# A two-layer transformer kernel: gate weights loaded first, later loads moved back, gate-row and key products over 128 rows

## The chip, the cores and the metric

The kernel runs on one core of one Trainium2 chip. The metric is the device time of one execution in microseconds (us). Before the change the median of three runs is 2478.57 us (2474.83 to 2481.1).

TensorE (PE) multiplies, with its weight loads shown as PEld; VectorE (DVE), ScalarE (ACT) and GpSimd (POOL) do the elementwise work; SyncE (SP) issues nearly all transfers (DMAs). Each engine works through its instructions in order.

## The reference, cut to what matters

The model has an mLSTM layer, a retrieval feed-forward layer, an attention layer, a second retrieval layer and a last hybrid layer with a feed-forward part. The change lies in the first: a gated recurrence over 256 tokens with 8 heads, query and key of 64 and value of 128 numbers a head.

```python
proj = x @ w_in                    # q, k, v, gates, output gate
ig = gate_i + b_if[0]; lf = log_sigmoid(gate_f + b_if[1])
b = cumsum(lf)
log_w = where(causal, b[t] - b[s] + ig[s], -inf)
m_t = maximum(log_inter, max(log_w, -1))
w = exp(log_w - m_t)
qk = einsum('bhtd,bhsd->bhts', q, k) * w
num = qk @ v + ...;  den = sum(qk) + ...
h = num / maximum(abs(den), exp(-m_t))
hn = layer_norm_per_head(h) * hn_g
out = (sigmoid(og) * hn) @ w_out
```

The kernel does all 256 tokens of a head at once: with M the running maximum of ig - b, the weight of source s for target t is exp(ig[s] - b[s] - M[t]) below the diagonal.

## The kernel before

Matrices are multiplied nearly in fp32 by splitting each operand into a rounded half (type fp32r, `hi`, by an ACT copy) and the rest (`lo`, by a subtraction on DVE or, where a call asks for it, POOL). `mm3` (lines 157 to 161) then makes three products: hi x hi, hi x lo, lo x hi. A weight slab of 1 MB comes from memory into one of three `raw` buffers (`prep`, line 131), is split in two parts into pools of 8 `hi` and 7 `lo` buffers, and is used by `linT` (weights stationary, output transposed) or `linN` (x stationary). A scheduler orders each engine's instructions by what is ready and by program order; pools decide when a load may start.

The mLSTM stage, `mlstm` (line 414), runs so:
- `load_x` (line 405) loads the transposed x in four pieces of 256 KB, each split in two. `trig_tables` (line 804) follows: rotation angles, needed much later, with a load of the positions, eight DVE operations and a sine on ACT.
- The gate weights (one slab of 512 KB) and four query/key slabs of 1 MB each go through `linT` with 24 and 4 x 48 products of 256 columns. Between them the gate chain runs on ACT and DVE over 32 rows (lines 447 to 469): absolute value, exponential, logarithm, a running sum (`Bc`), a running maximum (`M`), and both gate rows into `ab2`.
- Two PE transposes (line 481) turn `ab2` into per-token columns `tok`. Then `linN` makes the value product of four slabs, with 96 products of 512 columns (line 485); its `lo` halves are made on POOL.
- For each head, `head_a` (line 493) makes the gate rows: a fp32 product of the selector `sel` (8 rows, -1 in row h) with `M`, plus the causal mask, and a fp32 product of 64-row key and query. `head_b` (line 506) multiplies by the values and normalises. Products of the output gate and, later, of the output weights stand between the heads. `norm_heads` (line 529) normalises four heads and transposes them.
- `post_norm` (line 239) adds the residual and normalises; at its end the gain and shift rows `gr` and `br` (lines 283, 284) are applied on DVE. The retrieval layer begins with the slabs of `peer_w_q`.

The pool `mlw` holds two buffers each of the heads' work tiles and stays open to the end of the stage.

Of the kernel before, what the change touches and what calls it, by code (L numbers as in the profile page):

```python
# [17 lines left out]
OP = mybir.AluOpType  # L18
# [33 lines left out]
class Builder:  # L52
# [43 lines left out]
    def setup(self):  # L96
# [4 lines left out]
        nc.sync.dma_start(self.vecs, self.A["vecs"])  # L101
# [29 lines left out]
    def prep(self, name, s, lo_engine=None):  # L131
# [6 lines left out]
        self.nc.sync.dma_start(raw, src)  # L138
# [266 lines left out]
def load_x(B):  # L405
    nc = B.nc
    B.x32 = B.t(B.state, [P, KD, S], F32, "x32")
    for k in range(0, KD, 2):
        nc.sync.dma_start(B.x32[:, k:k + 2, :], B.A["xT"][:, k:k + 2, :])
        for i in range(k, k + 2):  # L410
            B.split(B.x32[:, i, :], B.xT[0][:, i, :], B.xT[1][:, i, :])


def mlstm(B):
# [4 lines left out]
    with B.pool("ml") as p, B.pool("mlw", 2) as w:  # L419
        for n, i in (("a_w_gate", 0), ("a_w_qk", 0)):  # L420
            B.prep(n, i, nc.gpsimd if i else v)
        nc.sync.dma_start(B.X, A["x"])
        qT = B.t(p, [P, 4, S], F32, "qT")
        kT = B.t(p, [P, 4, S], F32, "kT")
# [3 lines left out]
        sel = B.t(p, [8, 8, P], F32, "sel")  # L428
        nc.gpsimd.memset(sel, 0.0)
        nc.gpsimd.affine_select(out=sel, in_=sel, pattern=[[1, 8], [0, P]], compare_op=OP.not_equal, fill=-1.0,  # L430
                                base=0, channel_multiplier=-1)
        v.memset(va[:, :, :, 128:129], 1.0)
        hn = B.t(p, [P, D], F32, "hn")
        nc.sync.dma_start(hn, A["hn_g"].to_broadcast([P, D]))
        nc.gpsimd.tensor_scalar(hn, hn, 0.5, None, op0=OP.mult)
# [12 lines left out]
        e = B.t(p, [32, S], F32, "e")  # L448
# [10 lines left out]
        zero = B.t(p, [32, S], F32, "zero")  # L459
        v.memset(zero, 0.0)  # L460
# [17 lines left out]
        tok = B.t(p, [P, 2, 64], F32, "tok")
# [6 lines left out]
        acc = B.linN(B.xT, "a_w_v", lo_engine=nc.gpsimd)  # L485
# [7 lines left out]
        def head_a(h):  # L493
            r0, c = 64 * (h % 2), h // 2
            qk, lw = B.psum(), B.psum()
            ex = B.t(w, [P, 3 * P], F32, "ex")
            for sb in range(2):
                o = slice(sb * S, sb * S + S - sb * P)
                mm(lw[:, o], sel[:, h, :], M[0:8, sb * P:], start=True, stop=False)
                mm(lw[:, sb * S:sb * S + P], B.ident_b, B.smask_b, start=False, stop=True)  # L500
                mm(qk[:, o], kT[r0:r0 + 64, c, sb * P:(sb + 1) * P], qT[r0:r0 + 64, c, sb * P:], start=True, stop=True)
                act(ex[:, o], lw[:, o], AF.Exp, bias=tok[:, sb, h:h + 1])
            v.tensor_tensor(ex, ex, qk[:, :3 * P], op=OP.mult)
            pt[h] = ex
# [66 lines left out]
        B.accN(acc, [(oT, B.slab("a_w_out", s), 2 * s, 2) for s in (2, 3)], False, True)  # L571
        with B.pool("rows") as rows:
# [231 lines left out]
def trig_tables(B):  # L804
# [3 lines left out]
    with B.pool("tr") as p:  # L808
# [711 lines left out]
def build(tc, A, out, stages=ALL):  # L1520
    with ExitStack() as ctx:
# [56 lines left out]
```

## Time and profile before

| | |
|---|---|
| median of 3 runs | 2478.57 us |
| profiled execution | 2474.93 us, span 2472.0 us |
| PE busy | 2373.6 us, 96% of the span |
| DVE, ACT, POOL busy | 1627.4, 1230.4, 346.4 us |
| read and written | 457.99 and 34.60 MB |

Busy time of PE counts pipelined products from their start to their modelled end, so the spacing of starts says more than the duration of one. The granted clock (PEclk) is a share of 2.4 GHz: 0.50 is 1.2 GHz. A row of a timeline gives start, duration, engine, line, operation and tiles (output <- inputs), and in brackets the idle time of that engine before it and what ended it.

### The profile page before, as it was taken

Reading aid. Unit: us, or ns where it says so; the run is one execution under the profiler, and the core shown is the slowest. Engines: PE = TensorE matmul, PEld = TensorE weight load, DVE = VectorE, ACT = ScalarE, POOL = GpSimd, SP = SyncE. Lnnn points to the kernel's source line nnn. Section 1 sums busy time; section 2 is a strip of 40 time slices with the busy share of each in tenths; the row PEclk is TensorE's granted clock in tenths of the full one; section 3 lists DMA queues with packets and bytes.
Section 4 is the critical chain, followed back from the end, with each engine's and each line's share of the span. In section 5 each row is a group of like instructions: output and inputs, shape, how many; then the busy total and the mean of one; then the engine's idle time right before and its main releaser. Section 6 shows DMA issues by size and latency. Waiting matters only on the chain. (4 is left out here: it accounts for less than half of the span.)

```text
span 2472.0 us, 40796 instructions
## 1 busy us (share of the span) xinstructions
PE 2373.6 (96%) x16430; PEld 2167.0 (88%) x16430; DVE 1627.4 (66%) x3069; ACT 1230.4 (50%) x1813; POOL 346.4 (14%) x212
## 2 busy tenths in 40 slices
PE   7989999999999999989989999999999989999998
PEld 6779898889999998978989888999999888789998
DVE  5469995786666665656999566555555573459554
ACT  5455555444444444645455444444444464455442
POOL 5345000000000001445300000000000131313000
PEclk9989999999999999999999999999999999999999
DMA  7334577887677664433367766656655344224543
GB/s 258 120 110 150 226 282 268 293 326 264 251 263 273 255 227 148 154 137 131 144 239 280 258 236 218 227 200 208 218 208 201 137 162 160 81 86 161 198 149 108
DMA packets 134204, 495.22 MB, mean 200 GB/s; under 512 B 8064, under 2 KB 76032, under 8 KB 80896
## 3 DMA queue, kind: packets, MB, share of 16 engines
q1 hardware_dynamic: 129120, 458.55, 51.8%
q10 hardware_dynamic: 4896, 34.08, 3.4%
q8 instruction: 128, 2.10, 0.3%
q14 instruction: 60, 0.49, 0.1%
HBM read 457.99 MB, written 34.60 MB: 199 GB/s over the span
## 5 line engine op out<-in xcount | busy, mean ns | idle before, releaser
L78 ACT ACTIVATE hi<-raw 128x1024 fp32r<-128x1024 f32 (+1 forms) x754 | 771.3, 1044 | 838.8 <-PE ps L160 336.8
L129 DVE TENSOR_TENSOR lo<-raw,hi 128x1024 fp32r<-128x1024 f32 (+1 forms) x634 | 778.0, 1234 | 420.6 <-PE ps L161 254.2
L159 PE MATMUL ps<-s,hi 128*128 128x256 f32 x3248 | 923.5, 285 | 16.3 <-ACT hi L78 13.8
L160 PE MATMUL ps<-s,hi 128*128 128x256 f32 x3248 | 924.2, 285 | 2.1 <-DVE s L276 1.5
L161 PE MATMUL ps<-s,lo 128*128 128x256 f32 x3248 | 921.0, 284 | 5.3 <-DVE lo L129 5.3
L159 PEld LDWEIGHTS ps<-s,hi 128*128 128x128 f32 x3248 | 617.4, 190 | 22.6 <-ACT hi L78 14.2
L160 PEld LDWEIGHTS ps<-s,hi 128*128 128x128 f32 x3248 | 618.3, 190 | 7.4 <-issue 2.2
L161 PEld LDWEIGHTS ps<-s,lo 128*128 128x128 f32 x3248 | 617.9, 190 | 7.3 <-DVE lo L129 7.3
L129 POOL TENSOR_TENSOR lo<-raw,hi 128x1024 fp32r<-128x1024 f32 (+1 forms) x120 | 292.4, 2455 | 1340.6 <-ACT hi L78 1148.9
L159 PE MATMUL acc<-hi,ah 128*128 128x512 f32 x1024 | 400.6, 391 | 9.6 <-ACT ah L78 9.5
L160 PE MATMUL acc<-lo,ah 128*128 128x512 f32 x1024 | 401.0, 392 | 0.0
L161 PE MATMUL acc<-hi,al 128*128 128x512 f32 x1024 | 400.1, 391 | 0.0
L159 PEld LDWEIGHTS acc<-hi,ah 128*128 128x128 f32 x1024 | 193.1, 189 | 49.1 <-ACT ah L78 10.8
L161 PEld LDWEIGHTS acc<-hi,al 128*128 128x128 f32 x1024 | 193.0, 189 | 41.2 <-DVE al L129 0.7
L160 PEld LDWEIGHTS acc<-lo,ah 128*128 128x128 f32 x1024 | 193.0, 188 | 37.9
L129 DVE TENSOR_TENSOR al<-aw,ah 128x512 fp32r<-128x512 f32 x128 | 88.2, 689 | 54.9 <-ACT ah L78 54.8
L78 ACT ACTIVATE ah<-aw 128x512 fp32r<-128x512 f32 x128 | 80.1, 626 | 71.3 <-DVE aw L789 62.5
L789 DVE TENSOR_TENSOR aw<-g,wt 128x256 f32<-128x256 f32 x156 | 59.3, 422 | 39.4 <-ACT g L78 39.4
L756 PE MATMUL ps<-oh,o 128*128 128x128 f16 x512 | 65.1, 219 | 11.5 <-DVE oh L750 5.0
L78 ACT ACTIVATE st<-ps 128x512 f32<-128x512 f32 x128 | 66.6, 604 | 1.6 <-ACT pre L78 1.6
L78 ACT ACTIVATE g<-ps 128x512 f32<-128x512 f32 (+1 forms) x82 | 46.5, 567 | 39.1 <-PE ps L161 39.1
L757 PE MATMUL ps<-ol,o 128*128 128x128 f16 x512 | 64.7, 218 | 0.0
(461 smaller groups left out, 2433.6 us busy)
## 6 DMA issues: line engine op xcount, KB each, us to landing
raw<-in_peer_u SPq DMA_DIRECT2D x128, 1024.0 KB, 4.9
raw<-in_peer_v SPq DMA_DIRECT2D x128, 1024.0 KB, 4.9
wd<-st ACTq DMA_DIRECT2D x32, 1024.0 KB, 4.5
wt<-wd SPq DMA_DIRECT2D x32, 1024.0 KB, 6.1
raw<-in_w_ada SPq DMA_DIRECT2D x24, 1024.0 KB, 5.3
raw<-in_peer_w_q SPq DMA_DIRECT2D x16, 1024.0 KB, 4.9
raw<-in_ffn_gate SPq DMA_DIRECT2D x11, 1024.0 KB, 4.8
raw<-in_ffn_up SPq DMA_DIRECT2D x11, 1024.0 KB, 4.8
```

The source lines that it names most:

```text
L78: i = self.nc.scalar.activation(out, in_, func, **kw)
L129: (lo_engine or self.nc.vector).tensor_tensor(lo, src, hi.bitcast(F32), op=OP.subtract)
L159: mm(out, lhsT[0], rhs[0], start=first, stop=False)
L160: mm(out, lhsT[0], rhs[1], start=False, stop=False)
L161: mm(out, lhsT[1], rhs[0], start=False, stop=last)
L756: mm(ps[:, i * P:(i + 1) * P], o2[:, t // 2, :, t % 2], oh1[:, t // 2, :, t % 2], start=True, stop=False)
L757: w_last = mm(ps[:, i * P:(i + 1) * P], o2[:, t // 2, :, t % 2], ol1[:, t // 2, :, t % 2], start=False, stop=True)
L789: v.tensor_tensor(aw[:, sl].rearrange("p (g t) -> p g t", t=16), g[:, sl].rearrange("p (g t) -> p g t", t=16), wt[:, :, (j % 4) * 2 + i, : ...
```

## The change

- The load of the gate weights is issued first, on ACT's queue (`nc.scalar`) instead of SP's, from within `load_x`. The small constants `vecs` are loaded between the second and the third piece of x.
- The loads of the residual x, of the head gain `hn` and of the positions, with the rotation tables, come after the value product in program order; the two transposes of `ab2` as well. `hn` is scaled on DVE instead of POOL, and the value slabs' `lo` halves are made on DVE.
- The selector has 128 rows and type fp32r; `M` is split into two fp32r halves `Mp`, in 128 rows of which 32 are filled and the others zero. So one fp32 product over 8 rows becomes two fp32r products over 128 rows.
- Each head has a key tile of its own of 128 rows, of which the 64 of the other head are zero; the product with `qT` runs over 128 rows, still in fp32.
- Some tiles share memory (`e` with `ab`, `M` with `u`, `n` with `pi`, a one-column `zero`), and `mlw` is closed before `post_norm`, whose rows take its space.

```diff
@@ setup
-        nc.sync.dma_start(self.vecs, self.A["vecs"])
@@ prep
-    def prep(self, name, s, lo_engine=None):
+    def prep(self, name, s, lo_engine=None, queue=None):
-        self.nc.sync.dma_start(raw, src)
+        (queue or self.nc.sync).dma_start(raw, src)
@@ load_x
+    B.prep("a_w_gate", 0, None, nc.scalar)
     for k in range(0, KD, 2):
         nc.sync.dma_start(B.x32[:, k:k + 2, :], B.A["xT"][:, k:k + 2, :])
+        if k == 2:
+            nc.sync.dma_start(B.vecs, B.A["vecs"])
@@ mlstm
-    with B.pool("ml") as p, B.pool("mlw", 2) as w:
-        for n, i in (("a_w_gate", 0), ("a_w_qk", 0)):
-            B.prep(n, i, nc.gpsimd if i else v)
-        nc.sync.dma_start(B.X, A["x"])
+    with B.pool("ml") as p, ExitStack() as es:
+        w = es.enter_context(B.pool("mlw", 2))
+        B.prep("a_w_qk", 0)
-        kT = B.t(p, [P, 4, S], F32, "kT")
+        kT = B.t(p, [P, 8, S], F32, "kT")
+        nc.gpsimd.memset(kT, 0.0)
-        sel = B.t(p, [8, 8, P], F32, "sel")
-        nc.gpsimd.memset(sel, 0.0)
-        nc.gpsimd.affine_select(out=sel, in_=sel, ...
+        sel = B.t(p, [P, 8, P], F32R, "sel")
+        Mp = B.t(p, [P, 2, S], F32R, "Mp")
+        s32 = B.t(B.hi_p, [P, 8, P], F32, "hi")
+        nc.gpsimd.memset(s32, 0.0)
+        v.memset(Mp.bitcast(F32), 0.0)
+        nc.gpsimd.affine_select(out=s32, in_=s32, ...
+        act(sel, s32, AF.Copy)
-        hn = B.t(p, [P, D], F32, "hn")
-        nc.sync.dma_start(hn, A["hn_g"].to_broadcast([P, D]))
-        nc.gpsimd.tensor_scalar(hn, hn, 0.5, None, op0=OP.mult)
...
-        M = B.t(p, [32, S], F32, "M")
+        M = u
         v.tensor_tensor_scan(M, ab2[0:32, :], zero, 0.0, op0=OP.max, op1=OP.max)
+        B.split(M, Mp[0:32, 0, :], Mp[0:32, 1, :])
...
-                act(kT[:, c - 4, :], ps, AF.Copy, scale=0.125)
+                for r0 in (0, 64):
+                    act(kT[r0:r0 + 64, 2 * (c - 4) + r0 // 64, :], ps[r0:r0 + 64, :], AF.Copy, scale=0.125)
         B.linT(B.xT, "a_w_qk", range(4), ev_qk)
+        acc = B.linN(B.xT, "a_w_v")
+        trig_tables(B)
+        nc.sync.dma_start(B.X, A["x"])
+        hn = B.t(p, [P, D], F32, "hn")
+        nc.sync.dma_start(hn, A["hn_g"].to_broadcast([P, D]))
+        v.tensor_scalar(hn, hn, 0.5, None, op0=OP.mult)
...
-        acc = B.linN(B.xT, "a_w_v", lo_engine=nc.gpsimd)
...
-                mm(lw[:, o], sel[:, h, :], M[0:8, sb * P:], start=True, stop=False)
+                for i in range(2):
+                    mm(lw[:, o], sel[:, h, :], Mp[:, i, sb * P:], start=i == 0, stop=False)
-                mm(qk[:, o], kT[r0:r0 + 64, c, sb * P:(sb + 1) * P], qT[r0:r0 + 64, c, sb * P:], ...
+                mm(qk[:, o], kT[:, h, sb * P:(sb + 1) * P], qT[:, c, sb * P:], ...
...
+        es.close()
         with B.pool("rows") as rows:
@@ build
-        trig_tables(B)
         if "a0" in stages:
             mlstm(B)
```

On SP, at the start of the program before (`raw` is a weight slab, `s` the residual x, `pi` the positions, `gr` a row of the norm):

```order
L101 DMA vecs_84<-in_vecs 128x185
L409 DMA x_17_117<-in_xT 128x512 x4
L138 DMA raw_164<-in_a_w_gate 128x1024
L138 DMA raw_170<-in_a_w_qk 128x2048
L810 DMA pi_142<-in_positions 128x256
L422 DMA s_15_115<-in_x 128x2048
L138 DMA raw_298<-in_a_w_qk 128x2048
L138 DMA raw_359<-in_a_w_qk 128x2048
L434 DMA hn_192<-in_hn_g 128x1024
L138 DMA raw_420<-in_a_w_qk 128x2048
L283 DMA gr_1336<-in_ln_g 128x1024
```

SP at the same place after the change:

```order
L409 DMA x_17_116<-in_xT 128x512 x2
L411 DMA vecs_84<-in_vecs 128x185
L409 DMA x_17_116<-in_xT 128x512 x2
L137 DMA raw_150<-in_a_w_qk 128x2048
L137 DMA raw_279<-in_a_w_qk 128x2048
L137 DMA raw_340<-in_a_w_qk 128x2048
L137 DMA raw_403<-in_a_w_qk 128x2048
L824 DMA pi_610<-in_positions 128x256
L487 DMA s_15_114<-in_x 128x2048
```

The positions and the residual x now stand behind all query/key slabs, and the gate weights have left this queue. The row loads `gr` and `br` stand further on:

```order
L137 DMA raw_1471<-in_peer_w_q 128x2048
L137 DMA raw_1563<-in_peer_w_q 128x2048
L282 DMA gr_1361<-in_ln_g 128x1024
L283 DMA br_1362<-in_ln_b 128x1024
L137 DMA raw_1655<-in_peer_w_q 128x2048
```

Before, `gr` was the eleventh load and `br` stood among the output-gate slabs.

ACT at its start after the change (`s` are the rounded x pieces, `raw_117` the gate slab, `ab` and `lf` belong to the gate chain):

```order
L137 DMA raw_117<-in_a_w_gate 128x1024
L78 ACT_TABLE_LOAD
L78 ACTIVATE s_13_112<-x_17_116 128x256
L78 ACTIVATE hi_119<-raw_117 128x1024
L78 ACTIVATE s_13_112<-x_17_116 128x256 x7
L78 ACTIVATE hi_152<-raw_150 128x1024
L78 ACTIVATE hi_156<-raw_150 128x1024
L78 ACTIVATE ig_176<-ps_178,vecs_84 32x256
L78 ACTIVATE z_177<-ps_178,vecs_84 32x256
L78 ACTIVATE ab_205<-z_177 32x256
L78 ACTIVATE ab_205<-ab_205 32x256
L78 ACTIVATE sel_166<-hi_168 128x1024
```

Next stand a table load, the logarithm `lf`, and only then the split of the second query/key slab. Before, the gate split stood behind all eight x pieces.

PE at the first two heads before (`acc` are output-gate products):

```order
L499 MATMUL ps_642<-M_243,sel_186 128x256
L500 LDWEIGHTS ident_b_88
L500 MATMUL ps_642<-smask_b_91,ident_b_88 128x128
L501 MATMUL ps_641<-qT_181,kT_182 128x256
L501 MATMUL ps_641<-qT_181,kT_182 128x128
L499 MATMUL ps_654<-M_243,sel_186 128x256
L499 MATMUL ps_642<-M_243,sel_186 128x128
```

and after:

```order
L494 MATMUL ps_633<-ident_79,ab_43_218 128x64
L512 MATMUL ps_650<-Mp_167,sel_166 128x256 x2
L513 LDWEIGHTS ident_b_87
L513 MATMUL ps_650<-smask_b_90,ident_b_87 128x128
L514 MATMUL ps_649<-qT_160,kT_161 128x256
L514 MATMUL ps_649<-qT_160,kT_161 128x128
L512 MATMUL ps_664<-Mp_167,sel_166 128x256 x2
```

The transposes of `ab2` now stand directly ahead of the heads, and each gate-row product is a pair.

## Rows read from the trace of the kernel before

**Rows 1.** The page, busy time of one engine: us, share, instructions.

```profile
PE 2373.6 (96%) x16430; PEld 2167.0 (88%) x16430; DVE 1627.4 (66%) x3069; ACT 1230.4 (50%) x1813; POOL 346.4 (14%) x212
```

**Rows 2.** Timeline of all engines, 0 to 12 us: start, us, engine, line, operation.

```profile
4.74 1.42 ACT L78 ACTIVATE s<-x 128x256 fp32r<-128x256 f32 x4 [2.66 <-DMA x<-in_xT]
5.19 1.46 DVE L129 TENSOR_TENSOR s<-x,s 128x256 fp32r<-128x256 f32 x4 [4.11 <-ACT s L78]
...
8.23 0.72 ACT L78 ACTIVATE s<-x 128x256 fp32r<-128x256 f32 x2 [0.50 <-DMA x<-in_xT]
...
9.51 1.06 ACT L78 ACTIVATE hi<-raw 128x1024 fp32r<-128x1024 f32 x1 [0.55 <-DMA raw<-in_a_w_gate]
...
10.60 1.23 DVE L129 TENSOR_TENSOR lo<-raw,hi 128x1024 fp32r<-128x1024 f32 x1 [0.74 <-ACT hi L78]
```

**Rows 3.** Timeline of PE, 10 to 26 us.

```profile
10.62 0.58 PE L159 MATMUL ps<-s,hi 128*128 128x256 f32 x1 [10.62 <-ACT hi L78]
...
16.73 0.39 PE L159 MATMUL ps<-s,hi 128*128 128x256 f32 x1
...
22.41 0.28 PE L161 MATMUL ps<-s,lo 128*128 128x256 f32 x1
24.56 0.38 PE L159 MATMUL ps<-s,hi 128*128 128x256 f32 x1 [1.87 <-ACT hi L78]
...
25.82 0.39 PE L161 MATMUL ps<-s,lo 128*128 128x256 f32 x1 [0.76 <-DVE lo L129]
```

**Rows 4.** Timeline of ACT, 22 to 29 us.

```profile
22.48 0.47 ACT L78 ACTIVATE ig<-ps,vecs 32x256 f32<-32x256 f32 x1
...
28.18 1.28 ACT L78 ACT_TABLE_LOAD   x1
```

**Rows 5.** Timeline of all engines, 35 to 50 us.

```profile
35.37 16.39 POOL L129 TENSOR_TENSOR lo<-raw,hi 128x1024 fp32r<-128x1024 f32 x6 [5.70 <-DVE lf L458]
...
37.14 2.44 DVE L465 TENSOR_TENSOR ab<-ig,Bc 32x256 f32<-32x256 f32 x1
```

**Rows 6.** Timeline of PE, 47 to 48 us.

```profile
47.29 0.31 PE L481 MATMUL ps<-ident,ab 64*128 64x64 f32 x2 [3.42 <-POOL lo L129]
47.53 0.68 PE L159 MATMUL acc<-hi,s 128*128 128x512 f32 x1
```

**Rows 7.** Stretches: length, PE, PEld, DVE, ACT, POOL, PEclk, DMA share, GB/s.

```profile
49.00:51.00 2.00, 2.00 (x7) 1.54 (x6) 0.00 (x0) 1.07 (x2) 2.00 (x2) 0.50 0.94 377
76.00:78.00 2.00, 2.00 (x7) 1.43 (x7) 0.39 (x1) 0.37 (x1) 0.00 (x0) 0.50 0.68 283
100.00:108.00 8.00, 8.00 (x40) 6.22 (x39) 7.74 (x25) 3.86 (x7) 2.55 (x1) 1.00 0.29 106
```

**Rows 8.** Timeline of PE, 71 to 83 us.

```profile
71.47 0.69 PE L499 MATMUL ps<-M,sel 8*128 8x256 f32 x2
...
75.01 0.80 PE L159 MATMUL acc<-hi,s 128*128 128x512 f32 x1
...
82.04 0.40 PE L161 MATMUL acc<-hi,s 128*128 128x512 f32 x1
...
82.96 0.61 PE L511 MATMUL ps<-va,ex 128*128 128x129 f32 x4
```

**Rows 9.** Timeline of PE, 83 to 86 us: one head.

```profile
83.72 0.69 PE L499 MATMUL ps<-M,sel 8*128 8x256 f32 x2
84.35 0.23 PE L500 MATMUL ps<-smask_b,ident_b 128*128 128x128 bf16 x1
...
85.36 0.48 PE L499 MATMUL ps<-M,sel 8*128 8x128 f32 x2
85.77 0.23 PE L500 MATMUL ps<-smask_b,ident_b 128*128 128x128 bf16 x1
```

**Rows 10.** Timeline of SP, 100 to 165 us.

```profile
104.38 30.92 SPq L138 DMA_DIRECT2D raw<-in_peer_w_q  x4
```

**Rows 11.** Timeline of DVE, 100 to 165 us.

```profile
160.75 2.61 DVE L286 TENSOR_TENSOR s<-s,gr 128x1024 f32<-128x1024 f32 x2
```

More of the change, by code (lines that the diff above doesn't have):

```diff
@@ L427, in mlstm @@
         H = B.t(p, [P, 2, 8, P], F32, "H")
-        sel = B.t(p, [8, 8, P], F32, "sel")
-        nc.gpsimd.memset(sel, 0.0)
-        nc.gpsimd.affine_select(out=sel, in_=sel, pattern=[[1, 8], [0, P]], compare_op=OP.not_equal, fill=-1.0,
+        sel = B.t(p, [P, 8, P], F32R, "sel")
[3 more added lines that the diff above has]
+        v.memset(Mp.bitcast(F32), 0.0)
+        nc.gpsimd.affine_select(out=s32, in_=s32, pattern=[[1, 8], [0, P]], compare_op=OP.not_equal, fill=-1.0,
                                 base=0, channel_multiplier=-1)
+        act(sel, s32, AF.Copy)
         v.memset(va[:, :, :, 128:129], 1.0)
-        hn = B.t(p, [P, D], F32, "hn")
-        nc.sync.dma_start(hn, A["hn_g"].to_broadcast([P, D]))
-        nc.gpsimd.tensor_scalar(hn, hn, 0.5, None, op0=OP.mult)
         bif = B.vec("b_if")
@@ L447, in mlstm @@
         ab = B.t(p, [32, S], F32, "ab")
-        e = B.t(p, [32, S], F32, "e")
+        e = ab
         u = B.t(p, [32, S], F32, "u")
@@ L458, in mlstm @@
         v.scalar_tensor_tensor(lf, z, 0.0, lf, op0=OP.min, op1=OP.subtract)
-        zero = B.t(p, [32, S], F32, "zero")
-        v.memset(zero, 0.0)
+        zero1 = B.t(p, [32, 1], F32, "zero")
+        v.memset(zero1, 0.0)
+        zero = zero1.to_broadcast([32, S])
         ab2 = B.t(p, [64, S], F32, "ab2")
@@ L493, in head_a @@
         def head_a(h):
-            r0, c = 64 * (h % 2), h // 2
+            c = h // 2
             qk, lw = B.psum(), B.psum()
@@ L498, in head_a @@
                 o = slice(sb * S, sb * S + S - sb * P)
-                mm(lw[:, o], sel[:, h, :], M[0:8, sb * P:], start=True, stop=False)
+                for i in range(2):
+                    mm(lw[:, o], sel[:, h, :], Mp[:, i, sb * P:], start=i == 0, stop=False)
                 mm(lw[:, sb * S:sb * S + P], B.ident_b, B.smask_b, start=False, stop=True)
-                mm(qk[:, o], kT[r0:r0 + 64, c, sb * P:(sb + 1) * P], qT[r0:r0 + 64, c, sb * P:], start=True, stop=True)
+                mm(qk[:, o], kT[:, h, sb * P:(sb + 1) * P], qT[:, c, sb * P:], start=True, stop=True)
                 act(ex[:, o], lw[:, o], AF.Exp, bias=tok[:, sb, h:h + 1])
@@ L811, in trig_tables @@
         ang = B.t(p, [P, S], F32, "ang")
-        n = B.t(p, [P, S], F32, "n")
         v.tensor_copy(ang, pi)
+        n = pi.bitcast(F32)
         v.tensor_scalar(ang, ang, B.vec("inv_freq"), None, op0=OP.mult)
@@ L1530, in build @@
             B.nc.sync.dma_start(B.X, A["x"])
+            trig_tables(B)
         if "b0" in stages:
```

## The prediction, made before the changed kernel was run

> **What bounds the kernel now.** I read the page first. TensorE (PE) is busy for 96% of the span [rows 1], and the end is a chain of its products, so time is won only where PE stands still, runs at its lower clock, or does work that can be done in fewer passes. The edit touches the first stage alone (about 0 to 155 us), and behind that stage each engine's instructions stand in the same order before and after but for two row loads. So I read the stage in the timeline of all engines, then PE's own rows, then the stretches with their granted clock. Three losses stand out.
>
> At the start PE's first product waits until 10.62 for the rounded gate weights, which land behind all of x: the last x pieces are split at 8.23, and only at 9.51 are the gate weights [rows 2, 3]. Its 24 gate products end at 16.73, the 48 of the first query/key slab begin their last at 22.41, so each takes (22.41 - 16.73)/47 = 0.12 us, and then the second slab waits 1.87 us for ScalarE (ACT) and 0.76 us for VectorE (DVE) [rows 3].
>
> Before the value products PE waits 3.42 us [rows 6]. The row names GpSimd (POOL), but the two transposes behind it read what DVE's gate chain writes last, and that chain crawls while POOL splits value weights: a 32x256 subtraction takes 2.44 us beside POOL's 16.39 us of six splits [rows 5]. After the gap the granted clock is 0.50, which is 1.2 GHz [rows 7].
>
> At 75.01, with no gap before it, the clock falls again: 0.50 in the stretch from 76 [rows 7]. What PE did just before, from 71.47 on, was two heads' gate-row products with 8 contracted rows and key products with 64 [rows 8].
>
> **Part by part.** *Start.* The gate load goes out on ACT's queue beside x. The bytes up to the first slab are the same, so I take gain from the order alone. Estimate: gate lands at 5.7 (a choice between the first x split at 4.74 and its old 9.51), ACT's split of 1.06 ends at 6.8, DVE's of 1.23 at 8.0 [rows 2]. Before, the lo half was there at 10.60 + 1.23 = 11.83 and the 22 products behind it ran to 16.73, 0.22 each; 8.0 + 22 x 0.22 = 12.8 is the new end of the gate product, against 16.73. DVE's seven remaining x splits at 1.46/4 = 0.37 plus three casts keep up (8.0 + 3.1 = 11.1). Bounds: 11.5 where DVE alone sets it, 15 where gate lands at 7.8.
>
> *To the second slab.* ACT then has four gate passes of 0.47 like the first [rows 4], the rounding of the row selector (128x1024, 1.06 as in rows 2), a table load of 1.28 [rows 4], the logarithm 0.47, the second slab's split 1.06, and DVE its lo half 1.23: 1.9 + 1.06 + 1.28 + 0.47 + 1.06 + 1.23 = 7.0, with hand-overs 7.2. PE meanwhile needs 48 x 0.12 = 5.8, and waits the rest. So the third product of this slab starts at 12.8 + 7.2 = 20.0, against 25.82 [rows 3].
>
> *From there to the heads.* Still to do are 46 + 96 products at 0.12 and 96 value products at 0.23 (82.04 to 82.96 holds four [rows 8]): 17.0 + 22.1 = 39.1. I see no wait left among them: the gate chain no longer stands before the value products, POOL no longer splits beside it, and by the order each split's buffer is free about a slab (5.5 us) before PE needs its result. DVE gets eight value splits at 1.23 instead of POOL, 9.8 us, and the position tables; some 26 us of work in 40. The heads then begin at 20.0 + 39.1 = 59.1 instead of 71.47 [rows 8]: 12.4 won, less 0.24 for the two transposes that now follow the value products (47.29 to the next product at 47.53): **12.1**. The POOL fill of the wider key tile ends long before its first copy, and the selector fill too; both cost nothing.
>
> *Gate-row products.* A warm head spends 84.35 - 83.72 = 0.63 on the 256-column fp32 product and 85.77 - 85.36 = 0.41 on the 128-column one, 1.04 [rows 9]. Now each is two fp32r passes. For 256 columns that is 2 x 0.12 [rows 3]. For 128 columns no fp32r row exists; half of 0.12 is the floor, and 0.41/2 per pass the ceiling, as fp32 also comes as two instructions; I take the floor, as a pass of half the columns, and get 0.36. Saved 0.68 a head, 8 heads: 5.4. Bounds: 8 x (1.04 - 0.65) = 3.1 by that ceiling; 1.3 if each of the four passes also paid an unhidden weight load of 2167.0/16430 = 0.13 [rows 1]; and below nothing, 8 x (1.04 - 1.24) = -1.6, if the passes ran at the lower clock besides (2 x 0.36 + 4 x 0.13). Key products keep their columns and passes: 0.
>
> The Trainium skill (TensorE: Matmul & The Clock Gate, Back-to-back issue gap) states about 81 ns for a load and product pair of 128 columns; by it the term would be 8 x (1.04 - 0.24 - 0.16) = 5.1.
>
> Not all of this arrives. In the stretch from 100 to 108 DVE is busy 7.74 of 8.00 us [rows 7] with the head norms whose transposes PE must take in. Two heads' gain falls between the half gate that starts this work and those transposes: **-1.4** (bounds 0 to -1.4). Net **4.0**.
>
> *Clock at the heads.* 75.01 to 82.04 holds 14 products of 512 columns and one gate-row pair; warm that is 14 x 0.23 + 0.5 = 3.8 instead of 7.0. If the full rows keep the clock, **3.2** is won; bounds 0 and 3.2.
>
> *Loads moved back.* x for the residual, the norm gain and the positions follow the weights; the first two are wanted tens of us later. The two row loads g and b now follow the third peer_w_q slab on SP and need space of the pool that is closed earlier; SP issued the four such loads from 104.38 to 135.30 and the rows are first read at 160.75 [rows 10, 11], 25 us later. Cost 0.
>
> Sum: 12.1 + 4.0 + 3.2 = 19.3. The profiled execution took 2474.93 (span 2472.0 and 2.9 around it); 2474.9 - 19.3 = 2455.6. The median shown is 3.6 higher, and I carry that: **2459**.
>
> **Rivals.** *The clock falls anyway.* What speaks for it: zeros in 64 or 120 rows add no real work, and the fp32 key products still make slow passes. Against: after 83.72 single heads with the same products kept the full clock, and two heads together now last some 2.5 us, not 3.5. Then 3.2 is not won: 2462.
>
> The Trainium skill (same page, What's actually happening) ties the clock to how busy the engine was, with idle as the way down; PE was busy without a gap before 75.01, so the trace does not bear that out alone, and by it full rows would change nothing, which is this rival's 2462.
>
> *Gate first does not start PE sooner.* Loads of two queues share the bandwidth, x lands later by the gate's bytes, and the gate product ends at its old 16.73 or, at best, 15. At 16.73 it costs 3.9: 2463. For it: nothing of the bytes is saved. Against: ACT and DVE sat idle between x pieces.
>
> *DVE becomes the bound.* The value splits moved onto DVE run beside POOL's output-gate splits; where the two overlap, DVE passes are slowed as in rows 5. At twice the price, 8 x 1.2 = 9.6 more of DVE; if all of it reached PE, 2469. Against: two splits fit in a value slab's 24 x 0.23 = 5.5 even then.
>
> *Slower than before.* The g load waits on SP for the closed pool's space, and behind it stand the fourth peer_w_q slab and every later load; DVE, too, stops at the first use of g. Up to 25 us of hold it is free, from there each us costs PE one; with 19.3 won elsewhere it decides from a hold of 25 + 19 = 44 us on, and a hold of 55 us gives 2459 + 30 = 2489. For it: SP is in order. Against: the pool's last users are the last head's vectors, well before the output product ends.
>
> **How the numbers follow.** Forecast 0.62, clock 0.14, no earlier start 0.14, DVE 0.06, slower 0.04. A measurement of this kernel tells about 0.3% (7.4 us) from no change, so faster means under 2471: the first three cases and part of the fourth with some noise taken off, 0.90; same 0.06; slower 0.04. The range: below by the earliest gate product (1.3), no loss to DVE (1.4), no wait left at the second slab (7.2 - 5.8 = 1.4) and the 3 us by which runs of one kernel lie off their middle, rounded outward: 2451; above by both smaller rivals together (7.1) and that spread: 2469.
>
> **What would show it.** Right: the first product before 8 us and the gate product's end near 13; the second slab's third product near 20; no PE gap before the value products and no stretch at 0.50 there; the first gate-row product near 59; a granted clock of 1.00 through both heads; gate-row pairs of 0.24 and 0.12 to 0.16. Wrong: a 0.50 stretch after the first two heads, a gap in front of a value slab released by DVE, PE waiting at the head norm's transposes for longer than 1.4, or a late g row at the norm. If the stage shortens by 19 and the total does not, a later stage gave it back, which nothing here explains.

## The result, and the profile after

The changed kernel took 2452.28 us (median of 6 runs, 2449.77 to 2459.83) against 2479.84 us before (6 runs): ratio 0.9893, 95% interval 0.9874 to 0.9912. The forecast was 2459 in 2451 to 2469, faster with 0.90. The direction and the range held, but the median lies only 1.3 us above the lower end of the range: the gain was 27.6 us by the medians where 19.6 (2478.57 - 2459) were forecast. The profiled execution took 2451.36 us, span 2449.4.

The gain that the marks below show is won ahead of 140 us. The page's line of busy times, which answers to [rows 1]:

```profile
PE 2355.6 (96%) x16430; PEld 2158.1 (88%) x16430; DVE 1631.1 (67%) x3080; ACT 1231.2 (50%) x1818; POOL 324.2 (13%) x204
```

The share of PE is the same 96% on a shorter span: 18 us less busy time for the same 16430 instructions that the trace holds.

**The start.** Timeline of all engines of the changed kernel, the places of [rows 2, 3]:

```profile
5.90 0.42 ACT L78 ACTIVATE s<-x 128x256 fp32r<-128x256 f32 x1 [3.38 <-DMA x<-in_xT]
6.22 1.04 ACT L78 ACTIVATE hi<-raw 128x1024 fp32r<-128x1024 f32 x1
...
7.30 1.23 DVE L128 TENSOR_TENSOR lo<-raw,hi 128x1024 fp32r<-128x1024 f32 x1 [0.52 <-ACT hi L78]
...
7.32 0.58 PE L158 MATMUL ps<-s,hi 128*128 128x256 f32 x1 [7.32 <-ACT hi L78]
```

The gate weights are split at 6.22 instead of 9.51, x at 5.90 instead of 4.74: the two loads share the time, and the gate weights win more than x loses. Behind its first product PE then runs to the heads with two short waits only, of 0.47 and 0.90 us:

```profile
8.58 0.58 PE L160 MATMUL ps<-s,lo 128*128 128x256 f32 x1 [0.47 <-DVE lo L128]
...
13.43 0.37 PE L158 MATMUL ps<-s,hi 128*128 128x256 f32 x1
...
20.60 0.39 PE L160 MATMUL ps<-s,lo 128*128 128x256 f32 x1 [0.90 <-DVE lo L128]
...
59.70 0.33 PE L494 MATMUL ps<-ident,ab 64*128 64x64 f32 x2
59.96 0.50 PE L512 MATMUL ps<-Mp,sel 128*128 128x256 f32 x2
```

Counted from 7.32, the product at 13.43 is the 25th, the first of the first slab, so the gate product ends there, 3.3 us earlier than the 16.73 of [rows 3]; the second slab's third product comes at 20.60, before at 25.82; no wait stands between it and the transposes, where [rows 6] had 3.42 us; and the first gate-row product begins at 59.96 instead of 71.47 [rows 8], 11.5 us earlier.

**The heads.** Stretches of the changed kernel (columns as in [rows 7]); the 0.50 ahead of the heads and inside them is gone:

```profile
44.00:50.00 6.00, 6.00 (x28) 4.87 (x27) 1.02 (x1) 3.99 (x4) 4.26 (x2) 1.00 0.68 255
60.00:70.00 10.00, 10.00 (x60) 8.73 (x60) 3.32 (x13) 6.42 (x13) 6.08 (x3) 1.00 0.41 129
70.00:80.00 10.00, 10.00 (x58) 8.50 (x56) 4.72 (x12) 5.25 (x10) 6.53 (x3) 1.00 0.51 189
```

One head on PE in the changed kernel, to lay beside [rows 9], with the values' product ahead of it:

```profile
67.29 0.39 PE L526 MATMUL ps<-va,ex 128*128 128x129 f32 x2
67.43 0.48 PE L512 MATMUL ps<-Mp,sel 128*128 128x256 f32 x2
67.76 0.23 PE L513 MATMUL ps<-smask_b,ident_b 128*128 128x128 bf16 x1
67.82 0.87 PE L514 MATMUL ps<-qT,kT 128*128 128x256 f32 x4
68.55 0.44 PE L512 MATMUL ps<-Mp,sel 128*128 128x128 f32 x2
68.83 0.23 PE L513 MATMUL ps<-smask_b,ident_b 128*128 128x128 bf16 x1
```

Read starts, not lengths. The pairs take 67.76 - 67.43 = 0.33 and 68.83 - 68.55 = 0.28; before 0.63 and 0.41. The stretch of the mask and the keys between them takes 0.79 against 85.36 - 84.35 = 1.01.

**The end of the heads.** As a mark I take PE's transposes of the second half's head norm (six in a row, behind a wait for ACT). In the kernel before, and in the changed one:

```profile
135.65 1.94 PE L540 MATMUL ps<-ident,sg 128*128 128x128 f32 x6 [2.33 <-ACT sg L78]
```

```profile
114.15 1.79 PE L553 MATMUL ps<-ident,sg 128*128 128x128 f32 x6 [2.10 <-ACT sg L78]
```

21.5 us earlier: 11.5 up to the first gate-row product, 10.0 from there to the mark (64.18 became 54.19). The row loads g and b, which the slower rival watched, are issued at 110.38 and 110.76, and the first use is at 139.92 instead of 160.75 [rows 11], 20.8 us earlier: nothing was held. Timelines of SP and DVE:

```profile
110.38 0.33 SPq L282 DMA_DIRECT2D gr<-in_ln_g  x1
```

```profile
139.92 2.62 DVE L285 TENSOR_TENSOR s<-s,gr 128x1024 f32<-128x1024 f32 x2
```

### The profile page after: what moved, and what is told of

Its sections match the earlier page's. It is cut to its first block, busy times and chain, and to the rows that moved or that the text cites. A ratio compares the mean times of both kernels' runs of the same rounds, so it can differ in the third digit from the quotient of the medians.

```text
span 2449.4 us, 40793 instructions
## 1 busy us (share of the span) xinstructions
PE 2355.6 (96%) x16430; PEld 2158.1 (88%) x16430; DVE 1631.1 (67%) x3080; ACT 1231.2 (50%) x1818; POOL 324.2 (13%) x204
## 4 chain that ended last, share of the span: by engine, by line
PE 44%; DVE 3%; ACT 2%; issue 1%; DMA 1%; DVEq 0%; ACTq 0%; SPq 0%
PE ps L159 9%; PE ps L160 8%; PE ps L158 8%; PE acc L158 5%; PE acc L159 5%; PE acc L160 5%; DVE lo L128 1%; PE ps L1272 1%; ACT hi L78 0%; DVE sg L867 0%; PE acc L1285 0%; ACT s L78 0%; DMA wt<-wd 0%; PE acc L1158 0%; PE ps L770 0%
## 5 line engine op out<-in xcount | busy, mean ns | idle before, releaser
L128 DVE TENSOR_TENSOR lo<-raw,hi 128x1024 fp32r<-128x1024 f32 (+2 forms) x642 | 789.2, 1236 | 421.1 <-PE ps L160 255.4
L128 POOL TENSOR_TENSOR lo<-raw,hi 128x1024 fp32r<-128x1024 f32 (+1 forms) x112 | 271.3, 2437 | 1352.9 <-ACT hi L78 1177.7
```

Of the source, the lines that this page charges most:

```text
L128: (lo_engine or self.nc.vector).tensor_tensor(lo, src, hi.bitcast(F32), op=OP.subtract)
```

## The experiments

Two theories. *Rows*: the start's gain comes from the order of the loads and of the splits; in the heads, contracting 128 rows is what holds the clock and makes the products beside it cheaper. *Passes*: what matters in the heads is that a rounded pair replaces the fp32 product, and the clock fell for the waits ahead. The table gives, for each run's profiled execution, the start of the first gate-row product, the start of the transposes that mark the end, the time between, whether the clock fell between, and the ratio of the medians with its interval. Times in us.

| kernel | heads begin | mark | between | clock | ratio to before |
|---|---|---|---|---|---|
| before | 71.47 | 135.65 | 64.18 | falls | |
| changed | 59.96 | 114.15 | 54.19 | holds | 0.9893 [0.9874, 0.9912] |
| e1 loads alone | 58.69 | 123.09 | 64.40 | falls | 0.9937 [0.9922, 0.9953] |
| e2 heads alone | 67.69 | 124.32 | 56.63 | holds | 0.9953 [0.9941, 0.9966] |
| e3 pairs on 8 rows | 59.90 | 117.34 | 57.44 | holds | 0.9915 [0.9897, 0.9934] |
| e4 fp32 on 128 rows | 58.86 | 114.50 | 55.64 | holds | 0.9910 [0.9892, 0.9927] |
| e5 keys on 64 rows | 58.35 | 114.12 | 55.77 | holds | 0.9899 [0.9883, 0.9916] |
| e6 gate on SP's queue | 59.11 | 113.30 | 54.19 | holds | one run |
| e7 loads in front | 64.33 | 120.25 | 55.92 | holds | one run |
| e8 value halves on POOL | 61.82 | 123.11 | 61.29 | falls | one run |
| e9 before, value halves on DVE | 67.23 | 131.43 | 64.20 | falls | 0.9959 [0.9942, 0.9975] |
| e10 fp32 on 8 rows | 58.84 | 117.98 | 59.14 | holds | 0.9926 [0.9907, 0.9946] |
| e11 packed rows, three edits at the start | 62.25 | 114.60 | 52.35 | holds | 0.9886 [0.9866, 0.9907] |
| e12 packed rows, gate on SP's queue | 59.74 | 112.05 | 52.31 | holds | 0.9893 [0.9874, 0.9912] |

**e1, the loads and the order without the heads.** The changed kernel with

```diff
-                for i in range(2):
-                    mm(lw[:, o], sel[:, h, :], Mp[:, i, sb * P:], start=i == 0, stop=False)
+                mm(lw[:, o], sel[:, h, :], M[0:8, sb * P:], start=True, stop=False)
-                mm(qk[:, o], kT[:, h, sb * P:(sb + 1) * P], qT[:, c, sb * P:], start=True, stop=True)
+                mm(qk[:, o], kT[r0:r0 + 64, c, sb * P:(sb + 1) * P], qT[r0:r0 + 64, c, sb * P:], start=True, stop=True)
```

> The changed kernel with the heads of the kernel before: fp32 gate-row products on 8 rows, key products on 64 rows, no sel and Mp rounding, no memset of kT; the loads and the order as changed. Theory (contracted rows decide the heads: rows of 8 and 64 let the clock fall, and each change between row counts costs 0.1 to 0.2 us): the heads begin 11 to 12 us earlier than before, the granted clock still falls to 0.50 inside them although no wait of TensorE stands ahead, and the end of the heads is only 11 to 13 us earlier; about 2466 against 2479.8, ratio 0.994 to 0.995. Rival (the waits for the value slabs' halves brought the clock down, the rows have nothing to do with it): the granted clock stays at 1.00 through the heads and the end of the heads is 15 us earlier or more; 2462 or less, ratio 0.993 or less.

Measured: heads 12.8 us earlier than before, the mark 12.6, 2463.0 us. Stretches of this run, with the heads' first products at 58.69 and PE busy throughout:

```profile
56.00:60.00 4.00, 4.00 (x18) 2.75 (x17) 0.36 (x2) 3.10 (x5) 3.82 (x2) 1.00 0.72 262
60.00:64.00 4.00, 4.00 (x17) 2.43 (x15) 0.17 (x1) 2.99 (x6) 2.38 (x2) 0.86 0.67 240
64.00:67.00 3.00, 3.00 (x9) 2.38 (x9) 0.94 (x2) 0.37 (x1) 0.00 (x0) 0.50 0.09 36
```

The clock goes to 1.2 GHz with no idle of PE and no wait since 13.65 us. So the wait of [rows 6] is not needed for the fall in the heads, and the rival is out.

**e2, the heads without the loads.** The kernel before with wide `kT`, rounded `sel` and `Mp` and the pairs:

```diff
-                mm(lw[:, o], sel[:, h, :], M[0:8, sb * P:], start=True, stop=False)
+                for i in range(2):
+                    mm(lw[:, o], sel[:, h, :], Mp[:, i, sb * P:], start=i == 0, stop=False)
```

> The kernel before with only the heads changed: gate rows as rounded pairs on 128 rows, key products on 128 rows; loads and order as before, the values' halves on GpSimd still. Theory (contracted rows): the first heads start where they did (71.5 us, give or take 0.5), the clock falls at 49 to 51 behind the 3.42 us wait as before and not at 76 to 78; 8 heads at 0.7 to 0.9 us each and the clock make the end of the heads 7 to 10 us earlier; about 2471, ratio 0.996 to 0.997. Rival (the pairs save only what the forecast said, and the clock falls anyway): 4 to 5 us, ratio 0.998.

Measured: 2465.86 us. The theory's start was missed: the 3.42 us wait did not come back (the transposes begin at 45.13 without one) and the heads begin 3.8 us early, by a reordering that this edit brings along and that I did not follow up. Only the stretch between is the heads' own: 56.63 against 64.18, with 1.66 us of waits for `ex` at the first two heads. The clock held. The gains of e1 and e2 by the ratios, 0.0063 and 0.0047, make 0.0110 together; both at once made 0.0107.

**e3, pairs on 8 rows.** The changed kernel with

```diff
-                    mm(lw[:, o], sel[:, h, :], Mp[:, i, sb * P:], start=i == 0, stop=False)
+                    mm(lw[:, o], sel[0:8, h, :], Mp[0:8, i, sb * P:], start=i == 0, stop=False)
```

> The changed kernel, but the gate-row products contract the first 8 rows alone of the same two rounded tiles, still as a pair; key products stay on 128 rows. Theory (contracted rows): a switch between 8 and 128 rows costs 0.1 to 0.2 us at three places of a head, so the heads take 2 to 4 us more, and the clock may fall once inside them (3 us); 2455 to 2459, ratio 0.990 to 0.9915. Rival (passes decide: a pair of rounded passes in place of the fp32 passes is all there is to it): time of a head unchanged at 1.40 us from one L512 to the next head's, clock at 1.00, 2452, ratio 0.989.

Measured: 2457.76 us; heads 3.25 us longer. Same passes, same columns, fewer rows, and slower: one head's rows, with the values' product ahead of it,

```profile
68.10 0.39 PE L526 MATMUL ps<-va,ex 128*128 128x129 f32 x2
68.42 0.50 PE L512 MATMUL ps<-Mp,sel 8*128 8x256 f32 x2
68.85 0.23 PE L513 MATMUL ps<-smask_b,ident_b 128*128 128x128 bf16 x1
68.92 0.87 PE L514 MATMUL ps<-qT,kT 128*128 128x256 f32 x4
69.72 0.43 PE L512 MATMUL ps<-Mp,sel 8*128 8x128 f32 x2
70.08 0.23 PE L513 MATMUL ps<-smask_b,ident_b 128*128 128x128 bf16 x1
```

The pairs take 0.43 and 0.36 instead of 0.33 and 0.28, the step from keys to the second pair 0.80 instead of 0.73, the step from the values into the first pair 0.32 instead of 0.14: 0.07 to 0.18 us at each of the four steps that touch the 8 rows, 0.43 a head, 3.4 for eight heads. The clock did not fall, which that theory had left open.

**e4, one fp32 product on 128 rows.**

```diff
-                for i in range(2):
-                    mm(lw[:, o], sel[:, h, :], Mp[:, i, sb * P:], start=i == 0, stop=False)
+                mm(lw[:, o], sel[:, h, :], Mp[:, sb * P:], start=True, stop=False)
```

> The changed kernel, but the gate rows are kept in fp32: sel and the one row tile are not rounded, and one fp32 product over 128 rows (the tile's other rows are zero) takes the place of each rounded pair. Theory (contracted rows): the clock stays at 1.00 through the heads, and a head costs 0.1 to 0.4 us more than with pairs (fp32 passes over 256 and 128 columns, no switch of rows), 1 to 3 us in all, less some 0.5 us for the rounding that is gone; 2453 to 2455, ratio 0.9895 to 0.990. Rival (passes decide): each head gets back the kernel before's 1.04 us for its gate rows, 0.43 us more, and the clock falls at 60 to 70; 3.5 to 6 us, ratio 0.991.

Measured: 2454.25 us, heads 1.45 us longer, the clock holds: the theory of rows, and little is left for the passes. The heads begin 1.1 us earlier; e5 tells of that too.

**e5, keys on 64 rows.** The changed kernel with the second part of e1's diff alone.

> The changed kernel, but the key products contract 64 rows of a four-tile kT again, as in the kernel before; gate rows stay as rounded pairs on 128 rows. The run with 8-row pairs and 128-row keys kept the clock at 1.00 through the heads, the run with fp32 8-row gate rows and 64-row keys lost it at 60 to 70. Theory (the fp32 products on few rows bring the clock down, by themselves): the granted clock falls inside the heads, and the heads (54.2 us from the first gate-row product to the second half's transposes) take 3 to 6 us more; about 2456 to 2458, ratio 0.9905 to 0.9915. Rival (only gate rows and keys together leave too few rows at work): clock at 1.00, heads 1 to 2.5 us longer for switches between row counts; 2453 to 2455.

Measured: 2455.13 us; clock at 1.00, heads 1.58 us longer. The theory is wrong on the clock here and its rival right: 64-row keys beside 128-row pairs do not bring it down. And a surprise: the heads begin 1.61 us earlier than in the changed kernel, so the mark comes at 114.12 against 114.15, and by the mark the two kernels are level. ACT's rows for the slabs' splits, of the changed kernel and of e5:

```profile
15.42 1.04 ACT L78 ACTIVATE sel<-hi 128x1024 fp32r<-128x1024 f32 x1
...
18.10 3.89 ACT L78 ACTIVATE hi<-raw 128x1024 fp32r<-128x1024 f32 x4
```

```profile
15.53 1.04 ACT L78 ACTIVATE hi<-raw 128x1024 fp32r<-128x1024 f32 x1
```

And PE's rows of e5, at the start and at one head's keys:

```profile
11.58 0.41 PE L158 MATMUL ps<-s,hi 128*128 128x256 f32 x1
...
11.96 0.28 PE L160 MATMUL ps<-s,lo 128*128 128x256 f32 x1
```

```profile
66.99 0.92 PE L512 MATMUL ps<-qT,kT 64*128 64x256 f32 x4
67.84 0.44 PE L510 MATMUL ps<-Mp,sel 128*128 128x128 f32 x2
```

In the changed kernel the second slab's first split waits until 18.10 behind the rounding of `sel` and the logarithm; in e5, and in e1, e4 and e10 as well (14.67 to 15.39), it comes ahead of the logarithm, and the wait of 0.90 us at 20.60 is gone. In e1 and e5 the spacing of PE's products also goes from 0.21 to 0.12 us at 11.6 to 11.8, in the middle of the gate product, instead of at 13.43 (the granted clock in the rows reads 1.00 throughout). Nothing shows that this comes from the keys. Which of the edits turns ACT's order I did not separate: e4 and e10 keep the memset of the wide `kT`, e5 keeps the rounding, and e6 and e12 keep both, load the gate weights on SP's queue and have the early split too (16.15 and 15.22).

**e6, the queue.**

```diff
-    B.prep("a_w_gate", 0, None, nc.scalar)
+    B.prep("a_w_gate", 0)
```

> The changed kernel, but the gate weights are loaded on SP's queue, ahead of x, instead of ScalarE's. Theory (the order of loads decides, not the queue): TensorE's first product at 7.2 to 7.8 (7.32 in the changed kernel), end of the heads the same within 0.5 us. Rival (the second queue lets gate weights and x land side by side): x lands later by the gate weights' share and the first product begins at 8.5 to 9.5, all that follows 1 to 2 us later.

Measured: first product at 6.22, earlier than with the second queue, and the mark 0.85 us earlier; neither theory said that. By its order of instructions ACT splits the gate weights here ahead of all x. The second queue gave nothing. How much of the 0.85 us comes from the earlier first product and how much from the early split of the second slab named under e5 is not separated.

**e7, the loads in front again.**

```diff
         load_x(B)
         if "a0" in stages:
+            trig_tables(B)
...
         B.prep("a_w_qk", 0)
+        nc.sync.dma_start(B.X, A["x"])
```

(with `hn` in front as well).

> The changed kernel, but the loads of X, of hn and of the positions, and the trig tables' instructions, stand in front again as in the kernel before; the gate weights stay first. Theory (moving them back is worth something beside the gate-first order, for they stand on ScalarE, VectorE and SP ahead of the second slab): the waits at the second slab (1.87 us on hi, 0.76 us on lo in the kernel before) come back in part, heads begin 2 to 4 us later than at 59.96. Rival (they were free): heads begin within 0.5 us of 59.96.

Measured: first product at 7.25, but the heads begin at 64.33, 4.4 us later. Timeline of ACT and then of PE in this run:

```profile
18.17 0.42 ACT L78 ACTIVATE ang<-ang 64x256 f32<-64x256 f32 x1 [4.93 <-DVE ang L833]
...
19.55 1.28 ACT L78 ACT_TABLE_LOAD   x1
```

```profile
27.83 0.39 PE L158 MATMUL ps<-s,hi 128*128 128x256 f32 x1 [1.21 <-ACT hi L78]
...
29.09 0.39 PE L160 MATMUL ps<-s,lo 128*128 128x256 f32 x1 [0.75 <-DVE lo L128]
```

ACT stands still for 4.93 us at the tables' angle, with the slabs' splits queued behind it, and then loads another function table. The waits of [rows 3] come back, and the clock falls in the stretch behind them (0.72 in 30 to 36).

**e8 and e9, where the value halves are made.** e8 is the changed kernel, e9 the kernel before, each with this one line the other way:

```diff
-        acc = B.linN(B.xT, "a_w_v", lo_engine=nc.gpsimd)
+        acc = B.linN(B.xT, "a_w_v")
```

> The changed kernel, but the value slabs' lo halves are made on GpSimd again (2.4 to 2.7 us each in place of 1.2 us on VectorE). Theory (the six halves on GpSimd are what the values waited for): a wait of 2 to 4 us on POOL lo comes back before 50 us, the clock falls behind it, and the heads begin 3 to 5 us later. Rival (GpSimd starts earlier now, since nothing stands ahead of it, and keeps up): no wait, heads begin within 0.5 us of 59.96.

> The kernel before with one edit: the value slabs' lo halves are made on VectorE instead of GpSimd. Theory (the GpSimd halves hold up the values, and behind them the output gates' slabs): the wait of 3.42 us ahead of the transposes is gone, the clock doesn't fall at 49 to 51, heads begin 4 to 5 us earlier than 71.47; the fall inside the heads stays, since the products on few rows stay; end of the heads 4 to 6 us earlier, about 2475, ratio 0.9975 to 0.9985. Rival (VectorE, which carries the gate chain at that time, becomes the late one): waits on DVE lo of the same size, 0 to 2 us earlier, ratio 0.999 to 1.001.

Measured in e8: heads begin 1.9 us later, the mark 9.0 us later. GpSimd, ACT and PE of e8, a timeline each:

```profile
41.08 31.00 POOL L128 TENSOR_TENSOR lo<-raw,hi 128x1024 fp32r<-128x1024 f32 x13 [6.31 <-ACT hi L78]
```

```profile
65.65 1.06 ACT L78 ACTIVATE hi<-raw 128x1024 fp32r<-128x1024 f32 x1 [1.36 <-DMA raw<-in_a_w_og]
66.62 0.58 ACT L78 ACTIVATE va<-acc 128x512 f32<-128x512 f32 x1
...
68.63 0.82 ACT L78 ACTIVATE ex<-ps,tok 128x256 f32<-128x256 f32 x2
```

```profile
46.33 0.50 PE L159 MATMUL acc<-lo,s 128*128 128x512 f32 x1 [1.15 <-POOL lo L128]
...
69.14 0.69 PE L512 MATMUL ps<-Mp,sel 128*128 128x128 f32 x2 [4.11 <-ACT ex L78]
```

The wait on a POOL half that the theory named is there at 46.33, but with 1.15 us instead of 2 to 4, and the clock does not fall behind it; the heads begin 1.9 us later. The larger price, 7.1 of the 9.0 us, comes in the heads. The row at 69.14 names `ex`, but as I read these rows the cause sits further back. GpSimd works without a stop, so a `raw` buffer comes free late, the output gate's load lands late, ACT waits for it with the values' copy and the heads' exponential queued behind, and PE waits 4.11 us in the first two heads; the clock falls behind that gap. So both theories missed the place of the main price.

Measured in e9: heads begin at 67.23, 4.2 us earlier than before, as the theory had it. The clock falls in the heads again with no wait of PE ahead of it:

```profile
66.00:71.00 5.00, 5.00 (x24) 3.47 (x23) 0.55 (x1) 4.19 (x7) 4.49 (x2) 1.00 0.52 164
71.00:74.00 3.00, 3.00 (x9) 1.83 (x9) 0.55 (x1) 0.37 (x1) 0.20 (x1) 0.50 0.72 300
```

Its gain by the ratio, 10 us (6 to 14 by the interval), is larger than the 4.2 us at the mark; that is taken up below.

**e10, fp32 on 8 rows beside 128-row keys.** e1's first diff alone on the changed kernel.

> The changed kernel, but the gate rows are the kernel before's: fp32 sel and M on 8 rows, one product each, no rounding; key products stay on 128 rows. So far the clock fell in the heads with fp32 8-row gate rows beside 64-row keys, and held with rounded 8-row pairs beside 128-row keys, and with 128-row pairs beside 64-row keys. Theory A (fp32 products on 8 rows are enough to bring it down): the granted clock falls between 60 and 80, heads of 58 to 62 us against 54.2, 2457 to 2460. Theory B (it takes the 8-row and the 64-row products together): clock at 1.00, heads of 56.5 to 58.5 us for the switches and fp32 passes, 2454 to 2457.

Measured: 2461.79 us, clock at 1.00 in the heads: theory B on the clock. The heads took 59.14 us, more than B's 56.5 to 58.5: fp32 on 8 rows costs more than either part alone let me think.

**e11 and e12, a further step.** Only rows 0 to 7 of the selector are used, so hi and lo can stand in one tile and one product:

```diff
-        B.split(M, Mp[0:32, 0, :], Mp[0:32, 1, :])
+        B.split(M, Mp[0:32, :], Mp[32:64, :])
...
-                for i in range(2):
-                    mm(lw[:, o], sel[:, h, :], Mp[:, i, sb * P:], start=i == 0, stop=False)
+                mm(lw[:, o], sel[:, h, :], Mp[:, sb * P:], start=True, stop=False)
```

with a second -1 in `sel`, in row 32 + h. One head's gate rows in e12:

```profile
66.78 0.36 PE L513 MATMUL ps<-Mp,sel 128*128 128x256 f32 x1
66.98 0.23 PE L514 MATMUL ps<-smask_b,ident_b 128*128 128x128 bf16 x1
...
67.78 0.33 PE L513 MATMUL ps<-Mp,sel 128*128 128x128 f32 x1
67.95 0.23 PE L514 MATMUL ps<-smask_b,ident_b 128*128 128x128 bf16 x1
```

> The changed kernel with four edits: the rounded hi and lo gate rows stand in one tile (rows 0 to 31 and 32 to 63) and sel has its -1 in both, so one rounded product over 128 rows does what a pair did; the masks are made in a slot that nothing else is waiting for, so GpSimd's memset of kT runs before 5 us instead of at 10.33 beside VectorE; sel is rounded while ScalarE waits for the second slab; the gate weights go on SP's queue. Theory (passes saved on 128 rows come off TensorE's time one for one, and start waits are what the memset and the rounding cost): 0.25 to 0.3 us a head from the pairs, 2 to 2.4 us; heads begin 1 to 2 us earlier; end of the heads at 109.5 to 111.5 against 114.15; about 2448 to 2449, ratio 0.987 to 0.988. Rival (the heads are held by VectorE and ScalarE once TensorE needs less): the product's saving turns into waits for ex or sg, end of the heads at 112 to 113.5, 2451, ratio 0.9885.

> The changed kernel with two edits: one rounded product over 128 rows that holds the hi and the lo gate rows, in place of the pair, and the gate weights on SP's queue ahead of x; the masks and the memset stay where the changed kernel has them. In the run before this one the heads took 52.35 us with the packed product, but TensorE's first product came at 10.48, and 7.32 is the changed kernel's. Theory (the packed product is worth its 1.8 us and only the mask edit spoilt the start): first product at 6.2 to 6.4, heads begin at 58.9 to 59.3 and end at 111.2 to 111.8, against 114.15; about 2449.5 against 2452.3, ratio 0.987 to 0.989. Rival (the first product came late for the SP queue's sake or the packed rows'): first product after 8.5, end of the heads at 113 to 115, no better than the changed kernel.

Measured: e11 2453.16, e12 2451.84 us. The packed product gave what it should: 1.84 and 1.88 us in the heads, 0.23 a head. e11's start lost 2.3 us: with the masks in buffers of the slabs' `hi` pool, ACT's order puts seven x splits ahead of the gate weights and the first product came at 10.48. In e12 it came at 6.25, the mark at 112.05, 2.1 us ahead of the changed kernel's, though 0.25 later than the expectation; its heads begin at 59.74, 0.4 later than expected. Neither is shown to be faster than the changed kernel: e12's ratio is the same 0.9893 with the same interval. Two us are too little for these runs to tell.

## Why the prediction was right, point by point

*What decided it:* the direction rested on three terms of one sign, and all three came.

*Start and order to the heads: forecast 12.1, measured 11.5.* The marks were 12.8, 20.0 and 59.1 (59.3 with the two transposes) and came at 13.4, 20.6 and 60.0; the first 0.6 us runs through. Part of it is luck: the 22 products at 0.22 us that gave 12.8 are not a price of the gate product, for e5 goes over to 0.12 in the middle of it (11.58 and 11.96); in the kernel before and in the changed one the step only happens to fall on its end. The credit, too, was wrongly placed. The steps in a row of kernels are: before to e9 (value halves to DVE) 71.47 - 67.23 = 4.2; e9 to e7 (the gate weights first; the new heads come along) 67.23 - 64.33 = 2.9; e7 to changed (tables, x and hn moved back) 64.33 - 59.96 = 4.4. The prediction put "Cost 0" to the loads moved back and gave them no gain of their own; in this row they are the largest of the three. Its sum contained that gain unnamed, since it had ACT's chain to the second slab without the tables. The shares hang on the order in which they are taken: in the changed kernel the value halves are worth 1.9 at this mark (e8), not 4.2.

*Gate-row products: forecast 5.4 gross.* By e10 against the changed kernel: 59.14 - 54.19 = 5.0, with the clock at 1.00 in both. The size was right by luck, and the way to it was not. The pairs cost 0.33 and 0.28 us, not 0.24 and 0.12, since a pass is 0.12 but the first of a pair costs more: in e12 a single one takes 0.20 and 0.17. The two pairs make 0.61 a head, near the forecast's upper bound of 0.65, and by themselves save 8 x (1.04 - 0.61) = 3.4. What made up for it is the change of row counts. Going from 8 to 128 rows saves 3.25 us with pairs (e3) and 3.5 with fp32 (e10 against e4), of the same products; pairs instead of fp32 save only 1.45 (e4). The Trainium skill (TensorE: Matmul & The Clock Gate, Back-to-back issue gap) has 81 ns for a load and product of 128 columns, and the term came out at 5.1 by it; the measured pair of 128 columns is 0.28 us for the two, so the measurement differs and decides.

*Loss to DVE: forecast -1.4, measured 0.4.* At the first half's transposes PE waits 0.39 us (90.81), before and in e10 not at all; the 5.0 above are net of it. This and the next point are the step of the sum that was mis-sized.

*Key products: forecast 0, measured 1.6* (e5: 55.77 against 54.19). A 128-row key costs less than a 64-row one beside 128-row neighbours, 0.73 against 0.85 us a head to the next gate-row product (67.84 - 66.99 in e5).

*Clock at the heads: forecast 3.2.* e1 sums up as 54.19 + 4.95 (e10) + 1.58 (e5) = 60.7 without a fall, and took 64.40: 3.7. e10 and e5 each kept the clock, e1, e9 and the kernel before lost it, so it took both, the fp32 gate rows on 8 rows and the keys on 64. For the keys this is shown by the rows alone (e1 against e10); on the side of the gate rows e1 and e5 differ in the rows and in fp32 against pairs, and neither was run alone beside 64-row keys, so which of the two matters there stays open. That rests on one profile of each kernel: three of three with both lost it, and of the eleven with one or both at 128 rows only e8, behind its gap, did. The rival "the clock falls anyway" is out. The Trainium skill (same page, What's actually happening), which ties the fall to idle time, is not borne out by the rows of e1, where PE is busy without a gap ahead of the 0.50.

Sum of the stage: forecast 12.1 + 4.0 + 3.2 = 19.3, measured 11.5 + 10.0 = 21.5. The parts 5.0 + 1.6 + 3.7 make 10.2, which is e1 against the changed kernel by construction, since the 3.7 are what e1 leaves over; that the kernel before took 64.18 and e1 64.40 is the check.

*The other rivals:* gate first did start PE sooner (7.32); DVE did not become the bound, though e8 shows that an engine for the value halves can, with GpSimd; the row loads held nothing.

*From the profile to the median: 27.6 against 21.5 at the mark, and the forecast's carry of 3.6.* The 6 us above the mark's gain are not the forecast's doing; without them the median would be 2458.3. The two profiled executions differ by 23.6, and the carry was 4.9 before (2479.84 - 2474.93) but 0.9 after (2452.28 - 2451.36). The rest of the program has clock falls of its own, and they move. One place of the later layers, in the kernel before and in the changed one, 17 us apart in time:

```profile
2102.00:2110.00 8.00, 7.41 (x35) 4.53 (x33) 4.87 (x12) 4.42 (x10) 4.70 (x2) 0.96 0.47 186
2110.00:2120.00 10.00, 10.00 (x40) 7.34 (x40) 4.61 (x12) 6.19 (x16) 0.00 (x0) 0.52 0.01 2
```

```profile
2085.00:2093.00 8.00, 7.42 (x36) 4.36 (x35) 5.53 (x14) 4.84 (x14) 3.94 (x2) 1.00 0.36 138
2093.00:2103.00 10.00, 10.00 (x76) 8.54 (x75) 8.11 (x18) 7.96 (x20) 4.52 (x3) 1.00 0.09 20
```

The same program part runs at 0.52 in one execution and at 1.00 in the other, and PE's lead over before, counted between the same products, grows there from 18 to 22.5 us; it had been 22 at 160 us and 17 from 400 on. In e3's and e11's executions the fall is there, in e12's the lead jumps as in the changed kernel's. Nothing in the change touches that place. So a single profile's span is worth some 5 us either way, and the marks inside the stage are worth far more than the totals. Nor do the medians average it out for certain: in e1 to e5, e10 and e12 the median's gain is 0.3 to 4.7 us above the gain at the mark, in the changed kernel, e9 and e11 5.9 to 6.7. Why a kernel whose later instructions are the same should keep such an offset stays open.

## What to carry to other kernels

In these runs a product that contracts few rows was not cheap: padding its operands with zeros to 128 rows made the same products faster and the neighbours too, and kept the clock up. Padding one of the two, the gate rows or the keys, was enough for the clock, and with wide gate rows the wider keys as well are not shown to gain (e5 reaches the mark at the same time, by an earlier start). What fills the padding, and where it lands in the order, has to be counted. Look at which engine carries work that comes early and is wanted late (tables, gains, halves of weights): whatever it issues ahead of the first slabs is paid at the second slab, and a late helper engine is paid where its buffers are next needed. When an edit is costed by its stage, measure at a mark at the stage's end; totals here carry some 5 us that belong to other stages.

## What the runs showed of the hardware that was not expected

- Around products with 8 contracted rows among products with 128 each step costs 0.07 to 0.18 us more: into the 8-row pair 0.32 instead of 0.14, from the pair to the mask 0.43 instead of 0.33 (e3).
- A rounded pass of 128 columns behind another costs 0.28 - 0.17 = 0.11 us, one of 256 columns 0.33 - 0.20 = 0.13 (changed kernel against e12): half the columns, nearly the same time (e12's head above).
- The granted clock fell to 0.50 with PE busy throughout (e1 at 64, e9 at 71), and, where no gap of PE stood ahead, held in each kernel in which either the gate rows or the keys had 128 rows.
- In one stretch of the later layers, the same work ran at 0.52 and at 1.00 in different executions.
- VectorE's two splits of 128x1024 took 3.27 us beside GpSimd's making of the selector on 128 partitions (changed kernel, 12.00), and 2.36 beside that on 8 (e10, 11.95), as with none beside them (e5, 12.05). But in e10 it was GpSimd's select that took longer, 2.17 us (13.09) against 1.09 in the changed kernel (13.10) and 1.08 on 8 partitions in e1 (11.44). So one or the other was late, and the number of partitions is not shown to decide which.
